# Holding the next block's squares behind ScalarE's evictions in a hybrid GLA/pooling layer pair

## The chip, the core and the metric

The kernel runs on one core of one Trainium2 chip. That core has a matmul engine (PE, with PEld for its weight loads), VectorE (DVE), ScalarE (ACT), GpSimd (POOL) and a queue on SyncE (SP) that issues the DMAs. The engines run side by side, each through its own list of instructions in a fixed order, and wait for each other by semaphores. The metric is the time of one execution in device microseconds (us); lower is better.

## The reference, cut to what matters

Two layers run over 2176 tokens (128 of a prompt, 2048 of a sample) with 1024 channels, in float32. Layer 0 is a gated linear attention (GLA) beside a spatial gating unit, layer 1 a pooling mixer beside a short convolution. Both begin with a norm over the channels of each token, and the change touches only how the first layer's norm is scheduled:

```python
def rmsnorm(x, g):
    xf = x.astype(jnp.float32)
    y = xf * lax.rsqrt(jnp.mean(xf * xf, axis=-1, keepdims=True) + EPS)
    return (y * g.astype(jnp.float32)).astype(x.dtype)
...
        shift, scale, gate = adaln(cond, w_ada[l], b_ada[l])
        h = rmsnorm(x, norm_g[l]) * (1.0 + scale) + shift
...
            out, s_f, s_b = mix_even(h @ w_in_even[j], j, gla_init[j][0], gla_init[j][1])
```

For every token the squares of its 1024 channels have to be summed before the first product with `w_in_even` can begin.

## The kernel before, in words

Tokens lie along the free axis and channels on the 128 partitions, in KT = 8 slabs of 128 channels. Every float32 product is made of three passes (`mm3`): each operand is split into a rounded part (`hi`, `hh`) and a rest (`lo`, `hl`), and hi*hi, hi*lo and lo*hi are summed in PSUM. The split is made by ScalarE (L220, L405) and VectorE or GpSimd (L221, L406).

Layer 0 runs in four blocks of tokens, here called block 0 to 3 (512, 512, 512 and 640 tokens). They begin in the trace at about 27, 217, 398 and 575 us, and layer 0's projections end near 640 us. A block (`block1`) does, in this order: `make_h` for the 8 slabs (L405 on ACT writes `ring_hh`, L406 on DVE writes `ring_hl`); a token-major product of 272 columns (`gemm_tok(0, ...)`) whose tiles of 128 tokens are taken out of PSUM by DVE (L760, L761, the low-rank gate) and ACT (L764, `gl_v`); the q and k products (L777); another token-major product (L792); two products for the gating unit (`gl`: L806 on DVE, L809 on ACT with the sum of squares); then the channel-major products of the gates (L320 to L326, L845, L850). PSUM tiles of these products come from one pool of two buffers (`pg_g`), so the third tile of a product waits until the first has been taken out.

Beside these products run side jobs, advanced by one step at each `tick()`, that is after every second tile or every channel-major product. The GLA of each 128-token tile is one (`gla_tile`, L524 to L682): a chain over ACT (L552), DVE (L557, L568) and POOL (L568) with small matmuls (L580, L586, L605, L613), a large exponential on ACT (L623), DVE products with it (L627 to L634), and at its end a small tile `gl_ub` with one buffer: DVE writes a column of it (L673), ACT the rest (L674), SP stores it (L676), and the next tile's L673 waits for that store. The gating unit's mixer is another side job (L813 to L833), in which POOL scales four tiles (L821).

`prep_x` (L434) is the side job of the change. For the next block it loads the 8 slabs of x (L443, into `ring_xk`, 8 buffers, each free once `make_h` of the present block has read it), has ACT square them (L306 for the first, straight into `tmp_acc`; L309 for the seven others, into `tmp_px`, 4 buffers), adds them up (L310, on POOL for the blocks 1 to 3, on DVE for block 0), takes the reciprocal root (`rstd`, L286) and scales x by it (`make_t`, L390 on DVE).

The written order is not the order on the engines. The framework (`schedule_with_timeline_sim=True`, L1782) plays the program through a model of the engines and lets an instruction take an engine as soon as, in that model, its inputs and buffers are there; what is written earlier goes first among those that are ready. So a square whose slab has come in may be placed on ACT ahead of an eviction that was written before it. Once the lists are made they are fixed, and on the chip an instruction waits for the one ahead of it on its engine.

## Time and profile before

| what | value |
|---|---|
| median of 3 runs | 1852.43 us (1844.92, 1853.93, 1852.43) |
| profiled execution, its own time | 1848.17 us |
| its span | 1846.4 us |
| PE busy | 94% of the span |
| DVE, ACT, POOL busy | 65%, 45%, 40% |

The profiled execution's span is 1.8 us shorter than its time; what lies around the span is not touched here. A row of the timeline gives start, busy time, engine, source line, operation, output and inputs, and in brackets how long the engine had sat idle before it and what ended that. A row of the stretches gives, for a window of time, its length and the busy time of PE, PEld, DVE, ACT and POOL in it, each with its count of instructions, the granted PE clock as a share of 2.4 GHz, the share of the DMA engines and GB/s. Matmuls are pipelined, so a row's duration is longer than the distance between two starts.

### The profile page before, as it was taken

The page shows a single profiled execution, that of the slowest core. Times are in us where ns is not written, and L with a number is a line of the kernel's source. Part 1 is how long each engine was busy: PE and PEld are TensorE (multiplying, and loading weights), DVE is VectorE, ACT ScalarE, POOL GpSimd, SP SyncE. Part 2 cuts the span into 40 slices and gives each one's busy share as a digit, 9 for nine tenths or more (in the row PEclk, how much of TensorE's full clock was granted, in tenths as well). Part 3 has the DMA queues.
Part 4 walks back from the last instruction along what each step waited for, and adds up shares of the span by engine and source line. Part 5 has one row for each costly group of instructions (what it writes and reads, how often), then busy time and mean ns, then how long its engine had stood idle before and what let it go on. Part 6 is the DMA issues. An engine that isn't in the chain of part 4 may idle for free. (4 is left out here: it accounts for less than half of the span.)

```text
span 1846.4 us, 39586 instructions
## 1 busy us (share of the span) xinstructions
PE 1729.9 (94%) x15115; PEld 1585.2 (86%) x15115; DVE 1198.2 (65%) x2288; ACT 837.7 (45%) x1795; POOL 744.6 (40%) x793
## 2 busy tenths in 40 slices
PE   5998999999999999999999798899999999999996
PEld 4876788878888988987799787889998999999996
DVE  5457805860687079567766899996768375937653
ACT  4544524552455156345445454554445354534531
POOL 0432422241323024255555777764346234522322
PEclk9998999999999999999999899999999999999998
DMA  9767756575654535557554576598977697669753
GB/s 332 278 229 274 264 201 242 191 234 208 229 184 152 208 138 178 168 182 237 179 167 135 189 255 218 193 307 274 329 231 231 208 323 241 219 193 328 240 181 126
DMA packets 217629, 410.58 MB, mean 222 GB/s; under 512 B 24544, under 2 KB 70368, under 8 KB 217440
## 3 DMA queue, kind: packets, MB, share of 16 engines
q1 hardware_dynamic: 217440, 408.06, 66.0%
q8 instruction: 119, 1.95, 0.4%
q14 instruction: 70, 0.57, 0.1%
HBM read 312.13 MB, written 95.83 MB: 221 GB/s over the span
## 5 line engine op out<-in xcount | busy, mean ns | idle before, releaser
L251 PE MATMUL pg_g<-t_t,wh_hi 128*128 128x272 f32 (+1 forms) x1920 | 375.9, 293 | 16.5 <-ACT tu_U L1485 6.2
L251 PEld LDWEIGHTS pg_g<-t_t,wh_hi 128*128 128x128 f32 x1920 | 304.9, 191 | 20.1 <-ACT tu_U L1485 6.6
L251 PE MATMUL pg_g<-t_t,wh_lo 128*128 128x280 f32 (+1 forms) x960 | 275.9, 292 | 10.0 <-DVE wh_lo L221 7.9
L251 PE MATMUL pg_g<-ring_hh,wp_hi 128*128 128x512 f32 (+2 forms) x632 | 234.6, 371 | 2.9 <-DVE tmp_ev L845 2.6
L251 PE MATMUL pg_g<-ring_hh,wp_lo 128*128 128x512 f32 (+2 forms) x632 | 229.5, 363 | 0.6 <-DMA wp_lo<-dr_w16l 0.6
L251 PE MATMUL pg_g<-ring_hl,wp_hi 128*128 128x512 f32 (+2 forms) x632 | 229.9, 364 | 0.0
L220 ACT ACTIVATE wh_hi<-wh_raw 128x512 fp32r<-128x512 f32 x202 | 126.5, 628 | 172.9 <-PE pg_g L251 117.0
L251 PEld LDWEIGHTS pg_g<-t_t,wh_lo 128*128 128x128 f32 x960 | 181.5, 191 | 12.3 <-DVE wh_lo L221 9.3
L310 POOL TENSOR_TENSOR tmp_acc<-tmp_acc,tmp_px 128x512 f32<-128x512 f32 (+5 forms) x83 | 113.9, 1372 | 159.5 <-ACT tmp_px L309 136.3
L251 PE MATMUL pg_g<-wp_hi,ring_hh 128*128 128x256 f32 (+1 forms) x528 | 157.4, 298 | 9.8 <-ACT gl_v L764 5.5
L251 PE MATMUL px_x<-t_t,wh_hi 128*128 128x272 f32 (+1 forms) x768 | 155.1, 296 | 5.4 <-DVE tmp_ev L1308 3.7
L221 DVE TENSOR_TENSOR wh_lo<-wh_raw,wh_hi 128x512 fp32r<-128x512 f32 x147 | 128.8, 878 | 44.6 <-ACT wh_hi L220 35.8
L251 PE MATMUL pg_g<-wp_hi,ring_hl 128*128 128x256 f32 (+1 forms) x528 | 153.1, 291 | 2.1 <-DVE ring_hl L406 2.0
L251 PE MATMUL pg_g<-wp_lo,ring_hh 128*128 128x256 f32 (+1 forms) x528 | 152.7, 290 | 0.0
L251 PEld LDWEIGHTS pg_g<-ring_hh,wp_hi 128*128 128x128 f32 x632 | 120.9, 191 | 23.9 <-DVE tmp_ev L845 3.0
L568 POOL TENSOR_TENSOR gl_Z<-gl_Z 128x128 f32<-128x128 f32 x170 | 82.6, 505 | 145.1 <-DVE gl_Z L568 102.1
L251 PEld LDWEIGHTS pg_g<-ring_hh,wp_lo 128*128 128x128 f32 x632 | 120.8, 191 | 17.2 <-issue 0.8
L251 PE MATMUL pg_g<-o_oh,wh_hi 128*128 128x272 f32 (+2 forms) x448 | 130.1, 291 | 5.2 <-ACT o_oh L220 2.0
L251 PEld LDWEIGHTS pg_g<-ring_hl,wp_hi 128*128 128x128 f32 x632 | 120.7, 191 | 14.6 <-issue 0.5
L251 PE MATMUL pg_g<-o_oh,wh_lo 128*128 128x272 f32 (+2 forms) x448 | 130.1, 291 | 2.5 <-DVE wh_lo L221 1.4
L251 PE MATMUL pg_g<-o_ol,wh_hi 128*128 128x272 f32 (+2 forms) x448 | 130.2, 291 | 2.0 <-DVE o_ol L221 2.0
L251 PEld LDWEIGHTS px_x<-t_t,wh_hi 128*128 128x128 f32 x768 | 123.4, 192 | 7.8 <-DVE tmp_ev L1308 3.2
(302 smaller groups left out, 4333.0 us busy)
## 6 DMA issues: line engine op xcount, KB each, us to landing
wh_raw<-in_w_dram SPq DMA_DIRECT2D x132, 256.0 KB, 3.7
wh_hi<-dr_hl SPq DMA_DIRECT2D x108, 256.0 KB, 3.7
wh_lo<-dr_hl SPq DMA_DIRECT2D x108, 256.0 KB, 4.0
wp_raw<-in_w_ada_dram SPq DMA_DIRECT2D x32, 512.0 KB, 5.3
wh_hi<-dr_wo SPq DMA_DIRECT2D x48, 256.0 KB, 4.7
wh_lo<-dr_wo SPq DMA_DIRECT2D x48, 256.0 KB, 5.0
dr_hl<-wh_hi SPq DMA_DIRECT2D x36, 256.0 KB, 3.4
dr_hl<-wh_lo SPq DMA_DIRECT2D x36, 256.0 KB, 2.7
```

What stands on the lines that cost most here:

```text
L220: act(out=hi, in_=src, func=AF.Copy)
L221: (eng or lo_engine()).tensor_tensor(out=lo, in0=src, in1=hi.bitcast(F32), op=ALU.subtract)
L251: mm(out=out, lhsT=a, rhs=b, start=start and i == 0, stop=stop and i == n - 1, skip_group_check=resumed)
L310: eng.tensor_tensor(out=acc, in0=acc, in1=sq, op=ALU.add)
L568: (dve if i >= 2 or s < 4 else gps).tensor_tensor(out=dst, in0=dst, in1=bc(src), op=ALU.add)
```

## The change

`add_square` now returns the ACT instruction of the square. Each eviction by ACT in the first half of `block1` (L764, L777, L792, L809 by the numbers of before) is remembered in `evicted`, and for the blocks 1 to 3 each square is given an order-only dependency (`NoSync`: no semaphore) on the eviction that was written last before it: on ACT it can't be placed ahead of that one. In the text of `prep_x` the square of slab k - 4 is now written behind the load of slab k; for block 0 the code is as before.

```diff
--- before.py
+++ after.py
@@ -209,6 +209,14 @@
     ctile = const(cT, [P, KT, 2], "ct")
     ident = const(ident_d, [P, P], "ident")
 
+    evicted = [None]
+
+    def in_order(i):
+
+        if evicted[0] is not None:
+            tc.add_manual_dep(i.ins, evicted[0].ins.name, mybir.DependencyInfo(
+                mybir.DependencyClass.NoSync, mybir.DependencyReason.DATA), reason="order")
+
 
     lo_ctr = [0]
 
@@ -303,11 +311,12 @@
 
     def add_square(acc, x, n, first, eng, inplace=False):
         if first:
-            act(out=acc, in_=x, func=AF.Square)
+            i = act(out=acc, in_=x, func=AF.Square)
         else:
             sq = x if inplace else px_tile(n)
-            act(out=sq, in_=x, func=AF.Square)
+            i = act(out=sq, in_=x, func=AF.Square)
             eng.tensor_tensor(out=acc, in0=acc, in1=sq, op=ALU.add)
+        return i
 
     def sigmoid_(x, s):
         act(out=s, in_=x, func=AF.Exp, scale=-1.0)
@@ -436,14 +445,26 @@
         n = P * len(TILES[bi])
         acc = tmp.tile([P, 640], F32, tag="acc", bufs=1)[:, 0:n]
         xb[bi] = []
-        for k in range(KT):
+        def x_in(k):
             x = xk_tile(n)
             xb[bi].append(x)
             for c0, t0, w in cols(bi):
                 load(out=x[:, c0:c0 + w], in_=xT[k, :, t0:t0 + w])
-            add_square(acc, x, n, k == 0, gps if bi else dve)
-            if k % 2:
-                yield 1
+
+        if bi:
+            for k in range(KT + 4):
+                if k < KT:
+                    x_in(k)
+                if k >= 4:
+                    in_order(add_square(acc, xb[bi][k - 4], n, k == 4, gps))
+                if k % 2:
+                    yield 1
+        else:
+            for k in range(KT):
+                x_in(k)
+                add_square(acc, xb[bi][k], n, k == 0, dve)
+                if k % 2:
+                    yield 1
         yield 1
         r = tmp.tile([P, 640], F32, tag="r", bufs=1)[:, 0:n]
         yield from rstd(acc, n, r, bi == 0)
@@ -761,7 +782,7 @@
             dve.tensor_tensor(out=l4[:, :, 2, :], in0=lr, in1=hi.bitcast(F32), op=ALU.subtract)
             for j in (0, 3):
                 gps.tensor_copy(out=l4[:, :, j, :], in_=hi.bitcast(F32))
-            act(out=v[i][:, 0:240], in_=o[:, 32:272], func=AF.Copy)
+            evicted[0] = act(out=v[i][:, 0:240], in_=o[:, 32:272], func=AF.Copy)
             lr_t(i - 1)
 
         def lr_t(i):
@@ -774,7 +795,7 @@
 
         def qk0(c, a, b, o):
             for i in range(a // P, b // P):
-                act(out=qk[i][:, c // 2, c % 2, :], in_=o[:, i * P - a:(i + 1) * P - a],
+                evicted[0] = act(out=qk[i][:, c // 2, c % 2, :], in_=o[:, i * P - a:(i + 1) * P - a],
                     func=AF.Copy, scale=0.125 if c < 2 else 1.0)
 
         if bi == 0:
@@ -789,7 +810,7 @@
             if c == c0:
                 lr_t(nt - 1)
         for i, o in gemm_tok(1, 272, h, nt, bi == 0):
-            act(out=v[i][:, 240:512], in_=o, func=AF.Copy)
+            evicted[0] = act(out=v[i][:, 240:512], in_=o, func=AF.Copy)
         for i in range(nt):
             if TILES[bi][i] == 1:
                 Sf[0] = gl.tile([P, 2, P], F32, tag="Sf", bufs=3)
@@ -806,7 +827,7 @@
                 dve.tensor_copy(out=vs[:, i, 2 * u:2 * u + 2, :],
                                 in_=o.rearrange("p (a b) -> p a b", a=2))
                 junk = nw_tile(256)
-                act(out=junk, in_=o, func=AF.Square, accum_out=sq[:, i, u:u + 1])
+                evicted[0] = act(out=junk, in_=o, func=AF.Square, accum_out=sq[:, i, u:u + 1])
 
         def mix():
             v5, a5, r5 = (tmp.tile([P, 5], F32, tag=f"s{i}", bufs=2)[:, 0:nt] for i in range(3))
```

The lists of the engines differ between some 40 us and the end of layer 0's blocks; POOL, SP, DVE and ACT have the same rows as before from there on. The lines of the new file are shifted: L314 and L317 are the squares (L306, L309 before), L318 their sum (L310), L785 the eviction L764, L830 the eviction L809, L781 and L782 the pair L760 and L761, L694 to L697 the handling of `gl_ub` (L673 to L676), L644 is L623, L648 to L655 are L627 to L634, L842 is L821, L589 is L568 and L561 is L540.

ScalarE at the start of block 1, before: `tmp_acc` and `tmp_px` are the squares of block 2's x, `gl_v` the evictions of block 1's first product, `tmp_ev` a gate of block 0, `gl_ub` the GLA tile that is stored.

```order
L306 ACTIVATE tmp_acc_3371<-ring_xk_3372 128x512
L314 ACTIVATE tmp_ev_2619<-tmp_ev_2619 128x512
L674 ACTIVATE gl_ub_2638<-ps_s_2625 128x2x128
L309 ACTIVATE tmp_px_3377<-ring_xk_3375 128x512
L315 ACTIVATE tmp_ev_2619<-tmp_ev_2619 128x512
L309 ACTIVATE tmp_px_3460<-ring_xk_3458 128x512
L309 ACTIVATE tmp_px_3465<-ring_xk_3463 128x512
L764 ACTIVATE gl_v_2752<-pg_g_2784 128x240
L309 ACTIVATE tmp_px_3548<-ring_xk_3546 128x512
L764 ACTIVATE gl_v_2753<-pg_g_2815 128x240
```

The same place after the change:

```order
L322 ACTIVATE tmp_ev_2619<-tmp_ev_2617 128x512
L323 ACTIVATE tmp_ev_2619<-tmp_ev_2619 128x512
L644 ACTIVATE gl_Z_2379<-gl_Z_2379 128x1024
L695 ACTIVATE gl_ub_2638<-ps_s_2625 128x2x128
L324 ACTIVATE tmp_ev_2619<-tmp_ev_2619 128x512
L785 ACTIVATE gl_v_2752<-pg_g_2784 128x240
L785 ACTIVATE gl_v_2753<-pg_g_2815 128x240
L785 ACTIVATE gl_v_2754<-pg_g_2865 128x240
```

All eight squares have left this place (the L306 and three L309 above, four L309 behind), and the exponential of a GLA tile (L644, L623 before) has come in, which before stood ahead of `make_h`.

VectorE at the start of block 2, before: `gl_M` and `gl_D` belong to a GLA tile, `tmp_lrh` and `gl_lr` are VectorE's part of taking out the first product's tiles, `gl_ub` is the column that waits for a store.

```order
L589 TENSOR_TENSOR gl_M_4886<-pm_m_4821,gl_mask_525 128x640
L593 TENSOR_REDUCE gl_D_4589<-gl_M_4886 128x64 x2
L760 CAST tmp_lrh_4976<-pg_g_4951 128x32
L761 TENSOR_TENSOR gl_lr_0_4_547<-pg_g_4951,tmp_lrh_4976 128x2x16
L673 COPY gl_ub_5250<-gl_dec_5147 128x2
L760 CAST tmp_lrh_5007<-pg_g_4982 128x32
L761 TENSOR_TENSOR gl_lr_1_5_548<-pg_g_4982,tmp_lrh_5007 128x2x16
```

The same place after the change:

```order
L655 TENSOR_TENSOR gl_Z_4576<-gl_qk_2759,gl_Z_4576 128x512
L415 SCALAR_TENSOR_TENSOR ring_hl_4928<-ring_xk_3703,cst_ada_104,ring_hh_4927 128x512
L610 TENSOR_TENSOR gl_M_4886<-pm_m_4821,gl_mask_525 128x640
L614 TENSOR_REDUCE gl_D_4585<-gl_M_4886 128x64 x2
L694 COPY gl_ub_5250<-gl_dec_5147 128x2
L781 CAST tmp_lrh_4976<-pg_g_4951 128x32
L782 TENSOR_TENSOR gl_lr_0_4_547<-pg_g_4951,tmp_lrh_4976 128x2x16
L781 CAST tmp_lrh_5007<-pg_g_4982 128x32
L782 TENSOR_TENSOR gl_lr_1_5_548<-pg_g_4982,tmp_lrh_5007 128x2x16
```

The column of `gl_ub` has moved from behind the first tile's pair to ahead of it; behind block 1's last `ring_hl` the four instructions L648 to L655 stand in the same way ahead of the first pair.

GpSimd in block 1, where it scales the mixer's four tiles (`sg_vs`), before: `gl_Z` is the GLA chain.

```order
L540 MEMSET gl_Z_3694 128x512
L821 TENSOR_SCALAR sg_vs_3278<-sg_vs_3278,tmp_s_95_3795 128x512 x4
L568 TENSOR_TENSOR gl_Z_3694<-gl_Z_3694 128x32x4 x2
L568 TENSOR_TENSOR gl_Z_3694<-gl_Z_3694 128x16x8 x2
L568 TENSOR_TENSOR gl_Z_3694<-gl_Z_3694 128x8x16 x2
L568 TENSOR_TENSOR gl_Z_3694<-gl_Z_3694 128x4x32 x2
```

The same place after the change:

```order
L318 TENSOR_TENSOR tmp_acc_3371<-tmp_acc_3371,tmp_px_3541 128x512
L318 TENSOR_TENSOR tmp_acc_3371<-tmp_acc_3371,tmp_px_3700 128x512
L318 TENSOR_TENSOR tmp_acc_3371<-tmp_acc_3371,tmp_px_3705 128x512
L318 TENSOR_TENSOR tmp_acc_3371<-tmp_acc_3371,tmp_px_3781 128x512
L561 MEMSET gl_Z_3682 128x512
L318 TENSOR_TENSOR tmp_acc_3371<-tmp_acc_3371,tmp_px_3784 128x512
L842 TENSOR_SCALAR sg_vs_3278<-sg_vs_3278,tmp_s_93_3789 128x512 x4
L318 TENSOR_TENSOR tmp_acc_3371<-tmp_acc_3371,tmp_px_3913 128x512
L589 TENSOR_TENSOR gl_Z_3682<-gl_Z_3682 128x32x4 x2
L318 TENSOR_TENSOR tmp_acc_3371<-tmp_acc_3371,tmp_px_3916 128x512
L589 TENSOR_TENSOR gl_Z_3682<-gl_Z_3682 128x16x8 x2
```

The seven sums (`tmp_acc`) now stand here, five of them ahead of the scaling; before they stood at the start of the block. In SP's list the loads of x stand where they stood, within two places.

## Rows read from the trace of the kernel before

**Rows 1.** This is the page's line of busy times: us, share of the span and instructions of each engine.

```profile
PE 1729.9 (94%) x15115; PEld 1585.2 (86%) x15115; DVE 1198.2 (65%) x2288; ACT 837.7 (45%) x1795; POOL 744.6 (40%) x793
```

**Rows 2.** This is the view by stretches; the columns are explained above the change.

```profile
0.00:640.00 640.00, 600.03 (x6170) 502.26 (x6171) 355.52 (x813) 277.98 (x616) 178.68 (x241) 0.98 0.67 232
...
140.00:180.00 40.00, 34.09 (x346) 24.99 (x339) 30.25 (x64) 18.68 (x33) 8.46 (x8) 0.88 0.79 271
...
229.00:240.00 11.00, 8.77 (x82) 8.34 (x80) 1.72 (x10) 5.63 (x12) 10.30 (x14) 0.84 0.77 287
...
300.00:340.00 40.00, 39.64 (x500) 32.05 (x500) 25.46 (x61) 18.37 (x44) 11.90 (x15) 1.00 0.70 236
...
380.00:420.00 40.00, 36.18 (x486) 31.11 (x485) 24.60 (x56) 21.59 (x41) 21.56 (x30) 1.00 0.70 233
```

**Rows 3.** This is the view of waits, PE's from 0 to 640 us: who waited for whom, us in total, times, the longest.

```profile
PE pg_g L251 <- DVE ring_hl L406: 2.0, 5, 0.6
...
PE pg_g L251 <- ACT ring_hh L405: 1.7, 1, 1.7
...
PE pg_g L251 <- ACT gl_v L764: 5.5, 2, 3.3
```

**Rows 4.** This is the timeline of PE: the starts of block 0, block 1 and block 2, and two later matmuls of block 1 and one of block 2.

```profile
44.26 0.49 PE L251 MATMUL pg_g<-wp_hi,ring_hh 128*128 128x272 f32 x1 [1.72 <-ACT ring_hh L405]
...
231.86 0.39 PE L251 MATMUL pg_g<-wp_hi,ring_hh 128*128 128x272 f32 x1 [2.23 <-ACT gl_v L764]
...
232.25 0.43 PE L251 MATMUL pg_g<-wp_hi,ring_hl 128*128 128x272 f32 x1
...
235.61 0.29 PE L251 MATMUL pg_g<-wp_hi,ring_hl 128*128 128x272 f32 x1
...
411.38 0.39 PE L251 MATMUL pg_g<-wp_hi,ring_hh 128*128 128x272 f32 x1 [3.31 <-ACT gl_v L764]
...
411.61 0.29 PE L251 MATMUL pg_g<-wp_lo,ring_hh 128*128 128x272 f32 x1
```

**Rows 5.** This is the timeline of ACT, at the starts of block 0 and block 1.

```profile
42.99 0.61 ACT L306 ACTIVATE tmp_acc<-ring_xk 128x512 f32<-128x512 f32 x1
...
227.60 0.63 ACT L306 ACTIVATE tmp_acc<-ring_xk 128x512 f32<-128x512 f32 x1 [2.72 <-DMA ring_xk<-in_xT_dram]
...
228.66 0.37 ACT L674 ACTIVATE gl_ub<-ps_s 128x256 f32<-128x256 f32 x1
...
230.91 0.63 ACT L309 ACTIVATE tmp_px<-ring_xk 128x512 f32<-128x512 f32 x1 [0.34 <-POOL tmp_acc L310]
...
231.45 0.35 ACT L764 ACTIVATE gl_v<-pg_g 128x240 f32<-128x240 f32 x1
```

**Rows 6.** This is the timeline of ACT, at the start of block 2.

```profile
404.27 0.74 ACT L309 ACTIVATE tmp_px<-ring_xk 128x640 f32<-128x640 f32 x1 [1.73 <-DMA ring_xk<-in_xT_dram]
...
406.10 0.37 ACT L674 ACTIVATE gl_ub<-ps_s 128x256 f32<-128x256 f32 x1
...
409.13 0.74 ACT L309 ACTIVATE tmp_px<-ring_xk 128x640 f32<-128x640 f32 x1 [2.15 <-DMA ring_xk<-in_xT_dram]
...
410.98 0.35 ACT L764 ACTIVATE gl_v<-pg_g 128x240 f32<-128x240 f32 x1
```

**Rows 7.** This is the timeline of DVE, at the starts of block 1 and block 2.

```profile
218.06 0.17 DVE L627 COPY gl_dec<-gl_Z 128x2 f32<-128x2 f32 x1 [1.19 <-ACT gl_Z L623]
...
219.41 3.40 DVE L406 SCALAR_TENSOR_TENSOR ring_hl<-ring_xk,cst_ada,ring_hh 128x512 fp32r<-128x512 f32 x5
...
229.13 0.20 DVE L760 CAST tmp_lrh<-pg_g 128x32 fp32r<-128x32 f32 x1
...
406.52 0.18 DVE L760 CAST tmp_lrh<-pg_g 128x32 fp32r<-128x32 f32 x1
...
411.69 0.17 DVE L673 COPY gl_ub<-gl_dec 128x2 f32<-128x2 f32 x1 [4.76 <-DMA dr_ub<-gl_ub]
...
411.77 0.18 DVE L760 CAST tmp_lrh<-pg_g 128x32 fp32r<-128x32 f32 x1
```

**Rows 8.** This is the timeline of SP, the store of `gl_ub` at the start of block 2.

```profile
408.28 0.33 SPq L676 DMA_DIRECT2D dr_ub<-gl_ub  x1
```

**Rows 9.** This is the timeline of DVE and ACT at the start of block 3, behind which no block follows and so no squares stand.

```profile
586.59 0.16 DVE L673 COPY gl_ub<-gl_dec 128x2 f32<-128x2 f32 x1
...
587.93 0.19 DVE L760 CAST tmp_lrh<-pg_g 128x32 fp32r<-128x32 f32 x1
...
588.44 0.69 ACT L764 ACTIVATE gl_v<-pg_g 128x240 f32<-128x240 f32 x2 [3.29 <-DVE tmp_lrh L760]
```

**Rows 10.** This is the timeline of POOL and DVE in block 0: sums on POOL, and two slabs of `make_h` on DVE, one beside them and one behind.

```profile
46.65 4.35 POOL L310 TENSOR_TENSOR tmp_acc<-tmp_acc,tmp_px 128x512 f32<-128x512 f32 x3 [2.29 <-ACT tmp_px L309]
...
48.00 1.85 DVE L406 SCALAR_TENSOR_TENSOR ring_hl<-ring_xk,cst_ada,ring_hh 128x512 fp32r<-128x512 f32 x1
...
51.20 0.74 DVE L406 SCALAR_TENSOR_TENSOR ring_hl<-ring_xk,cst_ada,ring_hh 128x512 fp32r<-128x512 f32 x1
```

**Rows 11.** This is POOL's view of the tile `tmp_acc` from 0 to 640 us (duration in ns: least, median, most), and POOL's timeline in block 1.

```profile
L310 POOL TENSOR_TENSOR tmp_acc<-tmp_acc,tmp_px x21: 1264/1292/1623, 46.6 to 418.9; 128x512 f32<-128x512 f32 x14, 128x640 f32<-128x640 f32 x7
...
313.40 6.68 POOL L821 TENSOR_SCALAR sg_vs<-sg_vs,tmp_s 128x512 f32<-128x512 f32 x4
...
320.06 1.12 POOL L568 TENSOR_TENSOR gl_Z<-gl_Z 128x128 f32<-128x128 f32 x2
```

## The prediction

> **What bounds the kernel now.** I read the page's busy times first: PE is busy for 94% of the span [rows 1], so time is won only where PE stands idle or runs at its lower clock. Then the stretches: in the first 640 us, to which the change is confined, PE is busy for 600.0 us, so 40 us are idle, some of them before the first product [rows 2]. Then PE's waits there. Those with which the moved squares can have to do are three groups: 5.5 us in two waits for `gl_v` (L764), 1.7 us in one wait for `ring_hh`, 2.0 us in five waits for `ring_hl` [rows 3]. The timeline of PE gives them their places: 1.72 us at the start of block 0, 2.23 us at the start of block 1, 3.31 us at the start of block 2 [rows 4].
>
> The timeline of ACT shows why the two long ones last. At the start of block 1 the first square sits 2.72 us on a load of x, with the store tile `gl_ub` behind it, and the eviction L764 begins only when three more squares are done, one of them held by GpSimd's sum; it begins at 231.45 and PE goes on at 231.86 [rows 4, 5]. At the start of block 2 two squares sit 1.73 and 2.15 us on loads, and L764 begins at 410.98, PE at 411.38 [rows 4, 6]. So ACT's fixed order, and not a lack of ACT time, is the cause. Block 3 has no squares behind it: there L764 begins 0.5 us after DVE's L760, so it waits for nothing but its own tile [rows 9].
>
> An idle PE costs more than its gap where the granted clock falls behind it. After the 2.23 us of block 1 a matmul row of 272 columns lasts 0.43 us, from 235.61 on 0.29 us [rows 4], and the granted clock of 229 to 240 us averages 0.84 [rows 2], that is 1.2 GHz for about 3.5 us (11 x 0.16 x 2), a loss of some 1.8 us. After the longer gap of block 2 it doesn't fall: 1.00 over 380 to 420 us [rows 2], and the next row lasts 0.29 us [rows 4]. So I count a fall as likely but not sure.
>
> **The change part by part.** The sum is made against the profiled execution, 1848.2 us.
>
> Block 0: the first square stands ahead of the second half of `make_h` on ACT, from 42.99 for 0.61 us [rows 5], and PE waits 1.72 us for that half [rows 4]. With the square gone it is 0.5 us (the rows overlap a little). Bounds: 0, if the products wait for `ring_hl` instead; 2.3, if the clock that falls here too (its rows last 0.4 us and more) stays up. I take 0.5. Beside it the sums leave GpSimd here, which matters for DVE (below).
>
> Block 1: all squares leave the place between `make_h` and L764 (the first two fences of the change). The eviction is then bound by DVE's L760 and L761, which ACT follows as in block 3. DVE's L760 came at 229.13 [rows 7]. In its way come L627 to L634, four instructions that take 1.35 us (218.06 to 219.41) and stood ahead of the first `ring_hl` [rows 7]; they now stand behind the last. But for the same reason `ring_hl` can begin that much earlier, and it no longer waits 1.19 us for the exponential [rows 7]. I count this as even: L760 at 229.1, L764 0.5 us later and 0.4 us for it and its signal, as now, PE at 230.0 in place of 231.9: 1.9 us gained and 0.3 us of wait left, so the clock should stay up, which is 1.8 us more. Together 3.7. Bounds: 0.5, if the 1.35 us come on top and the clock falls all the same; 4.0, the whole wait and the fall.
>
> Block 2: here something else is late next. On DVE the column of `gl_ub` (L673) now stands ahead of the first L760 (the second pair of fences). Before, it waited 4.76 us for the store of the GLA tile ahead of it and then ran at 411.69, but the first tile's pair had gone at 406.52, so only the second tile was held, until 411.77 [rows 7]. Now both are held, with everything behind them on DVE, and PE's third tile waits for them. The store is issued at 408.28 [rows 8], after ACT has written the tile at 406.10 [rows 6], and lands 3.4 us later (408.28 to 411.69). ACT gets to the tile sooner: it waited 1.73 us for x and squared for 0.74 [rows 6], 2.5 us together. The exponential L623 now stands in between, so I count 2.3 of it. With a store that much earlier L673 runs at 409.4, L760 at 409.5, L764 0.5 later, and PE goes on at 410.4 in place of 411.4: 1.0 us of the 3.3. Bounds: -1.2, if the store isn't earlier at all (411.8 for L760, 412.6 for PE); 3.3. In block 3, with no loads in the queue, L673 waits for nothing [rows 9], which shows that it need not be late.
>
> What takes on the squares: eight in each of three blocks move to the last evictions L809 of the gating unit. ACT is busy for 18.4 of the 40 us there (300 to 340) [rows 2], and the loads came in long before, so ACT has room. GpSimd is the tighter one. It took the seven sums while DVE was all but idle (1.72 of 11 us) [rows 2]; now five of them stand ahead of the scaling L821, and two among the first steps of the GLA chain (the third pair of fences). At 1.29 us each [rows 11] four of these come after the last L809 and push L821, which began at 313.40, back by up to 5.2 us, less what ACT's own order gave it in wait; I estimate 2 to 3. The first step of the chain behind it, at 320.06 [rows 11], moves by that and one sum more, up to 4 us. PE is idle there for only 0.4 of 40 us [rows 2], and the fixed order moves the GLA's small matmuls back as well, so most of it is hidden by the products in between; if that cover is gone it is 4 us in each of three blocks, 12 in all.
>
> The sums also slow DVE. `ring_hl` lasts 1.85 us beside a sum and 0.74 us without [rows 10]. The Trainium skill has a rule for this (SBUF — State Buffer, section "Who interferes with whom"): a VectorE instruction with two inputs in SBUF and a GpSimd instruction that reads SBUF hold a common port in turn, each for its whole length. The trace agrees, 1.85 against 0.74 us; by the rule as it stands each of the seven sums could hold DVE for its 1.29 us, 9 us in a block, and the sum below would end as in the second rival. By the rows, each collision costs DVE 1.1 us. In block 0 that is won back by `make_h` (one or two collisions, 1 to 2 us of DVE, on which PE waits little). In the new place DVE is busy for 25.5 of 40 us [rows 2], so perhaps four of seven sums collide, 4 us of DVE out of 14.5 idle. For crowding on GpSimd and DVE together I charge 1.5 us; bounds 0 and 16 (12 for the late chain, 4 for DVE).
>
> Between 140 and 180 us PE stands idle for 5.9 us, and the granted clock of 0.88 costs another 4.8 (40 x 0.12) [rows 2]. These are waits of the GLA and of the conditioning weights in the fixed order, which the change shuffles here more than anywhere. It can remove or add; I take 0, bounds -8 (won) and +6 (lost).
>
> The loads: in SP's list they stand where they stood. That half of the change I cost at nothing.
>
> Sum: 0.5 + 3.7 + 1.0 - 1.5 = 3.7 us won of 1848.2, or 0.2%. The profiled execution is one of four that are known: with the three runs shown (1844.9, 1852.4, 1853.9) their mean is 1849.9, and the median of the runs is 4.3 above the profiled one. I set the base at 1849.9 and predict 1846.
>
> **The rivals.**
>
> First, the waits change owner: DVE's pairs, held by L627 to L634 in block 1 and by the store in block 2, come as late as the evictions did. For it speaks that L673 has waited 4.76 us here already; against it that ACT's first wait for x, which made the store late, is gone. Then 0.5 + 0.5 + 0 - 1.5 is no gain: 1850.
>
> Second, slower: the late GLA chain. Five sums ahead of L821 and the collisions with DVE delay the chain by 4 us or more, and PE, whose order is fixed, stands at the first small matmul of the chain in each block. The point from which it decides is the cover: the wait shows only when the chain is later than the model that made the order takes it to be. Against it, the model knows the sums, and PE waited 0.4 us in this stretch before. Price: up to 12 to 16 us, less the 5.2 won at the block starts, and in the middle some 8 lost: 1858.
>
> Third, more is won than the starts: with fewer sums in the way of `make_h` and another order, the 10.7 us (5.9 + 4.8) lost from 140 to 180 us go largely. For it speaks that waits of this kind are missing in the same stretch of blocks 1 and 2 (1.00 from 300 to 340 us [rows 2]); against it, the change doesn't touch their cause. Then 3.7 + 8: 1838.
>
> That the order does not do what it says is ruled out for the squares by the lists, and holds for the loads.
>
> **How the numbers follow.** The forecast of 1846 has 0.5, the first rival 0.2, the second and the third 0.15 each. The likeliest's own range is 1841 to 1850. The range that should hold 8 in 10 reaches to the third rival with its own spread below and to the middle of the second above, and takes in that runs of one kernel lie 9 us apart: 1834 to 1858. About 0.5%, 9.3 us, is what a measurement of this kernel can tell from no change. Below 1843 on a base of 1852.4 lie most of the third rival and a fifth of the forecast: faster 0.25. Above 1861.7 lies the upper part of the second: slower 0.12. The rest, 0.63, is within.
>
> **What would show it.** Right: PE's wait for `gl_v` at the start of block 1 under 0.6 us and no fall of the clock behind it; at block 2 a wait of 2 to 2.6 us whose releaser is no longer a late ACT but DVE's L760 behind `gl_ub`; L405 at block 0 half a microsecond earlier; PE's idle time from 300 to 340 us under 1.5 us. Wrong: a wait of 2 us or more at block 1 with DVE as the releaser (first rival), PE idle at L586, L605 or L641 for over 2 us in the stretches after the moved sums (second), or the stretch from 140 to 180 us with a clock of 1.00 (third). A difference behind 640 us, where nothing is moved, would show that I have taken the change's reach too small.

## The result and the profile after

The changed kernel takes 1862.9 us, the median of 6 runs (1859.52 to 1868.42); the kernel before took 1849.66 beside it. The ratio over all runs (not exactly that of the two medians) is 1.0077, with a 95% interval of 1.0059 to 1.0094: slower by 14 us (11 to 17). The forecast was 1846, the range 1834 to 1858: the sign was wrong and the time lies outside. The profiled execution took 1859.52 us.

First the page's busy times, which answer to [rows 1], then the stretches of [rows 2], with two more; of these the one from 180 to 229 us is shown for the kernel before too.

```profile
PE 1733.8 (93%) x15115; PEld 1587.7 (85%) x15115; DVE 1216.6 (65%) x2288; ACT 835.9 (45%) x1795; POOL 751.6 (40%) x793
```

```profile
0.00:640.00 640.00, 592.34 (x6058) 493.85 (x6059) 369.83 (x813) 274.23 (x608) 186.85 (x241) 0.97 0.65 227
140.00:180.00 40.00, 38.09 (x405) 28.43 (x405) 32.91 (x70) 20.97 (x40) 16.80 (x19) 0.96 0.74 254
180.00:229.00 49.00, 44.59 (x483) 36.34 (x482) 42.86 (x73) 28.14 (x49) 21.06 (x20) 0.93 0.86 301
229.00:240.00 11.00, 8.72 (x123) 8.05 (x122) 5.84 (x17) 0.63 (x2) 2.84 (x7) 0.84 0.65 213
300.00:340.00 40.00, 37.79 (x513) 30.73 (x513) 26.11 (x58) 22.41 (x52) 21.73 (x22) 1.00 0.67 230
380.00:420.00 40.00, 36.56 (x424) 31.06 (x423) 31.64 (x70) 20.58 (x41) 16.00 (x21) 0.96 0.68 228
580.00:600.00 20.00, 16.38 (x293) 13.52 (x295) 18.82 (x37) 12.97 (x28) 8.38 (x10) 1.00 0.40 145
```

```profile
180.00:229.00 49.00, 47.74 (x477) 39.01 (x476) 43.20 (x78) 28.08 (x52) 21.35 (x25) 0.99 0.75 258
```

PE is idle for 7.7 us more of the first 640 us than before (640 - 592.34 against 640 - 600.03). Over the whole execution PE has the same 15115 matmuls; the span is 11.3 us longer (1857.7 against 1846.4), and PE's busy time 3.9 us (1733.8 against 1729.9). So most of the loss is waiting, and the rest is the same work taking longer, beside a granted clock of 0.97 in place of 0.98 in these 640 us. PE's waits from 0 to 640 us show for what:

```profile
PE pg_g L259 <- DVE ring_hl L415: 6.6, 11, 1.8
...
PE ps_s L792 <- POOL gl_lr L784: 3.7, 2, 2.2
PE ps_s L662 <- DVE sg_vs L851: 3.5, 1, 3.5
...
PE ps_s L792 <- DVE gl_ub L694: 2.3, 1, 2.3
PE ps_s L682 <- ACT gl_o L674: 2.2, 1, 2.2
PE ps_s L671 <- ACT gl_kT L665: 2.2, 1, 2.2
PE pg_g L259 <- ACT ring_hh L414: 2.1, 1, 2.1
PE ps_s L848 <- ACT gl_kT L665: 2.1, 1, 2.1
```

The wait for `gl_v`, 5.5 us in [rows 3], is gone, as the change meant. In its place stand waits of 2 to 3.5 us each, for the transposed `lr` at the block starts (L792), for the mixer's rows (`sg_vs`), for the GLA chain (`gl_o`, `gl_kT`), and for `ring_hl`, 6.6 us against 2.0.

To see where the time goes I measure from block to block, between the last evictions of q and k (L777 before, L798 after), on ACT's timeline: before, then after.

```profile
74.29 0.76 ACT L777 ACTIVATE gl_qk<-pg_g 128x128 f32<-128x128 f32 x4
...
266.16 0.78 ACT L777 ACTIVATE gl_qk<-pg_g 128x128 f32<-128x128 f32 x4 [4.66 <-PE pg_g L251]
...
445.38 0.79 ACT L777 ACTIVATE gl_qk<-pg_g 128x128 f32<-128x128 f32 x4 [5.46 <-PE pg_g L251]
...
634.10 0.45 ACT L777 ACTIVATE gl_qk<-pg_g 128x128 f32<-128x128 f32 x2 [2.25 <-PE pg_g L251]
```

```profile
73.30 0.76 ACT L798 ACTIVATE gl_qk<-pg_g 128x128 f32<-128x128 f32 x4
...
268.11 0.79 ACT L798 ACTIVATE gl_qk<-pg_g 128x128 f32<-128x128 f32 x4 [4.66 <-PE pg_g L259]
...
450.01 0.79 ACT L798 ACTIVATE gl_qk<-pg_g 128x128 f32<-128x128 f32 x4 [5.45 <-PE pg_g L259]
...
648.69 0.45 ACT L798 ACTIVATE gl_qk<-pg_g 128x128 f32<-128x128 f32 x2 [2.25 <-PE pg_g L259]
```

End to end, block 0 to 1 takes 191.9 us before and 194.8 after, 1 to 2 takes 179.2 and 181.9, 2 to 3 takes 188.4 and 198.3. All three are longer, the last by ten. Behind block 3 nothing is lost: from its last q and k eviction to the end of the span it is 1211.9 us before and 1208.6 after. PE's timeline at the start of block 3 after, where [rows 9] showed nothing late:

```profile
592.32 0.39 PE L259 MATMUL pg_g<-wp_hi,ring_hl 128*128 128x272 f32 x1 [0.87 <-DVE ring_hl L415]
...
598.70 0.52 PE L259 MATMUL pg_g<-wp_hi,ring_hl 128*128 128x272 f32 x2 [1.83 <-DVE ring_hl L415]
...
601.77 0.48 PE L792 MATMUL ps_s<-cst_ident,gl_lr 128*128 128x128 f32 x1 [1.51 <-POOL gl_lr L784]
```

VectorE is late there. It is busy for 18.82 of the 20 us from 580 to 600; the first `ring_hh` comes at 585.46, and the first L781 at 601.12, 15.7 us behind it (before 12.1, from 575.83 to the 587.93 of [rows 9]); whether the loss lies in that, the experiments show. A level of the GLA chain of block 2's last tile (L578, L589) stands among its `ring_hl`:

```profile
586.21 1.02 DVE L415 SCALAR_TENSOR_TENSOR ring_hl<-ring_xk,cst_ada,ring_hh 128x512 fp32r<-128x512 f32 x2 [0.70 <-ACT ring_hh L414]
587.14 0.69 DVE L578 TENSOR_TENSOR gl_L<-gl_qk,gl_L 128x512 f32<-128x512 f32 x1
587.75 0.49 DVE L589 TENSOR_TENSOR gl_Z<-gl_Z 128x128 f32<-128x128 f32 x2
...
601.12 0.28 DVE L781 CAST tmp_lrh<-pg_g 128x32 fp32r<-128x32 f32 x2
```

What has moved ahead of that shows best on PE's timeline of block 0: the row sums of the next x (L283 and L284 before, L291 and L292 after) among the mixer's tiles (L827, L848). Before, then after:

```profile
128.12 1.16 PE L827 MATMUL ps_s<-sg_wst,sg_vs 128*128 128x128 f32 x8
147.28 0.40 PE L283 MATMUL ps_s<-tmp_nw,cst_ones_r 128*128 128x512 f32 x1
...
151.37 1.05 PE L827 MATMUL ps_s<-sg_wst,sg_vs 128*128 128x128 f32 x8
...
172.23 1.16 PE L827 MATMUL ps_s<-sg_wst,sg_vs 128*128 128x128 f32 x8
```

```profile
167.34 1.05 PE L848 MATMUL ps_s<-sg_wst,sg_vs 128*128 128x128 f32 x8
...
170.79 0.50 PE L291 MATMUL ps_s<-tmp_nw,cst_ones_r 128*128 128x512 f32 x1
```

Before, the row sum is behind the mixer's first tile; after, behind its last, 97 us behind the last q and k eviction of the block in place of 72 (170.79 - 74.1, 147.28 - 75.1). With it goes the scaling of x on VectorE (L390, L399); in block 2 it begins 101 us behind that eviction in place of 79:

```profile
525.06 7.49 DVE L390 SCALAR_TENSOR_TENSOR ring_xk<-ring_xk,cst_gs,tmp_r 128x512 f32<-128x512 f32 x16
```

```profile
551.98 0.74 DVE L399 SCALAR_TENSOR_TENSOR ring_xk<-ring_xk,cst_gs,tmp_r 128x512 f32<-128x512 f32 x1
...
553.07 5.13 DVE L399 SCALAR_TENSOR_TENSOR ring_xk<-ring_xk,cst_gs,tmp_r 128x128 f32<-128x128 f32 x11
```

The reason is in the diff, and the prediction passed over it. The loop over the loads runs KT + 4 times in place of KT and yields at every second, so the preparation has two steps more ahead of its row sums. That this alone moves them, the first experiment shows.

### The profile page after: what moved, and what is told of

Its sections match the earlier page's. It is cut to its first block, busy times and chain, and to the rows that moved or that the text cites. A ratio compares the mean times of both kernels' runs of the same rounds, so it can differ in the third digit from the quotient of the medians.

```text
span 1857.7 us, 39591 instructions
## 1 busy us (share of the span) xinstructions
PE 1733.8 (93%) x15115; PEld 1587.7 (85%) x15115; DVE 1216.6 (65%) x2288; ACT 835.9 (45%) x1795; POOL 751.6 (40%) x793
## 5 line engine op out<-in xcount | busy, mean ns | idle before, releaser
L259 PE MATMUL pg_g<-ring_hl,wp_hi 128*128 128x512 f32 (+2 forms) x632 | 229.1, 362 | 0.0
L318 POOL TENSOR_TENSOR tmp_acc<-tmp_acc,tmp_px 128x512 f32<-128x512 f32 (+5 forms) x83 | 113.5, 1367 | 164.3 <-ACT tmp_px L317 157.3
L589 POOL TENSOR_TENSOR gl_Z<-gl_Z 128x128 f32<-128x128 f32 x170 | 85.1, 519 | 143.7 <-DVE gl_Z L589 105.3
```

Of the source, the lines that this page charges most:

```text
L259: mm(out=out, lhsT=a, rhs=b, start=start and i == 0, stop=stop and i == n - 1, skip_group_check=resumed)
L318: eng.tensor_tensor(out=acc, in0=acc, in1=sq, op=ALU.add)
L589: (dve if i >= 2 or s < 4 else gps).tensor_tensor(out=dst, in0=dst, in1=bc(src), op=ALU.add)
```

## The experiments

Two theories. A: the two added steps cost, by the late row sums and what hangs on them. B: the held squares and their sums cost, where they now stand among the mixer and the GLA chain. The lists settle a third, that the distance between load and square costs: squares written four loads late, with no hold and no added step, leave every engine's list as it was, row for row but for the numbers of buffers. So the distance does nothing by itself; with the hold it does something else, as the second group of runs shows. The differences below are worked out from each run's ratio to the kernel before, times 1849 us, with the 95% interval.

**The two halves apart.** The first kernel is the one before with two steps more, the second the changed one without them.

```diff
 two_steps_only (against the kernel before)
-        yield 1
+        for _ in range(3 if bi else 1):
+            yield 1
         r = tmp.tile([P, 640], F32, tag="r", bufs=1)[:, 0:n]
 hold_without_steps (against the changed kernel)
-                if k % 2:
+                if k % 2 and k < KT:
                     yield 1
```

> The kernel before, with nothing of the change but its length: the preparation of the next x yields two times more ahead of its reciprocal root, as it does in the changed kernel. No square is held, no load is issued earlier. Theory A (the two more steps are the loss: they push everything behind them, the row scale, the modulation of x and by them the GLA chains of the last tiles, into the starts of the next blocks): PE waits for ring_hl and for the transposed lr at the start of block 3 (2 to 3 us each, as in the changed kernel), the gl_v waits of blocks 1 and 2 stay, and the time is 8 to 16 us above the kernel before. Theory B (the loss comes from the squares and sums that now run among the mixer and the GLA chain): the time is within 3 us of the kernel before.

> The changed kernel, without the two more yields: the squares are still written four loads late and held behind ScalarE's evictions, but the preparation is as long as in the kernel before. Theory A: the gl_v waits are gone, PE does not wait at the start of block 3, and the time is 1 to 6 us below the kernel before (the 5.5 us of gl_v waits and their clock, less crowding). Theory B: the PE waits of the changed kernel in block 0 (3.5 us at L662 for sg_vs, 2.2 us at L682) and at 519 us stay, and the time is 6 to 13 us above the kernel before.

Measured: 1855.7, ratio 1.0050 (1.0033 to 1.0068), +9.2 us, as theory A said; and 1854.6, ratio 1.0034 (1.0020 to 1.0049), +6.3 us, as theory B said. In two_steps_only the row sum of block 0 stands behind the mixer's last tile, as in the changed kernel (at 172.63 us). Both theories hold, each for its part, and the parts add up to 15.5 against the 14.2 of the whole change. In two_steps_only the start of block 3 is that of the changed kernel, wait by wait, though no square has moved:

```profile
591.54 0.40 PE L251 MATMUL pg_g<-wp_hi,ring_hl 128*128 128x272 f32 x1 [0.88 <-DVE ring_hl L406]
...
597.91 0.52 PE L251 MATMUL pg_g<-wp_hi,ring_hl 128*128 128x272 f32 x2 [1.85 <-DVE ring_hl L406]
...
600.99 0.46 PE L772 MATMUL ps_s<-cst_ident,gl_lr 128*128 128x128 f32 x1 [1.51 <-POOL gl_lr L764]
```

In hold_without_steps the row sums are back in their place but their input is late: GpSimd's timeline in block 2, and PE's wait.

```profile
500.63 6.30 POOL L842 TENSOR_SCALAR sg_vs<-sg_vs,tmp_s 128x512 f32<-128x512 f32 x4
...
507.67 1.62 POOL L318 TENSOR_TENSOR tmp_acc<-tmp_acc,tmp_px 128x640 f32<-128x640 f32 x1
...
514.94 1.59 POOL L318 TENSOR_TENSOR tmp_acc<-tmp_acc,tmp_px 128x640 f32<-128x640 f32 x1
```

```profile
518.60 0.44 PE L291 MATMUL ps_s<-tmp_nw,cst_ones_r 128*128 128x384 f32 x1 [2.91 <-ACT tmp_nw L228]
```

Three of the sums stand behind the scaling of the mixer's rows (L842). The last ends at 516.5, and only then can ACT and GpSimd split the result for PE, which stands idle for 2.91 us. GpSimd's split begins at 518.62, 69 us behind the block's last q and k eviction; in the kernel before it began 44 us behind it (490.45 - 446.2).

**Where the squares stand.** hold_at_each_load writes each square behind its load again; hold_first_products takes, beyond that, the hold from the later evictions.

```diff
 hold_at_each_load (against the changed kernel)
-            for k in range(KT + 4):
-                if k < KT:
-                    x_in(k)
-                if k >= 4:
-                    in_order(add_square(acc, xb[bi][k - 4], n, k == 4, gps))
+            for k in range(KT):
+                x_in(k)
+                in_order(add_square(acc, xb[bi][k], n, k == 0, gps))
 hold_first_products (against hold_at_each_load)
-            evicted[0] = act(out=v[i][:, 240:512], in_=o, func=AF.Copy)
+            act(out=v[i][:, 240:512], in_=o, func=AF.Copy)
-                evicted[0] = act(out=junk, in_=o, func=AF.Square, accum_out=sq[:, i, u:u + 1])
+                act(out=junk, in_=o, func=AF.Square, accum_out=sq[:, i, u:u + 1])
```

> The order alone: each square is written right behind its load as in the kernel before, and held behind the last eviction written. Four squares come to stand between the sets of the mixer's rows instead of eight behind them. Theory A: as the kernel without the two steps, 1 to 6 us below the kernel before. Theory B: nearly the same crowding, 5 to 12 us above it. A third theory (the loads of x, or their distance from the squares, matter): PE waits for a DMA in front of a square's reader somewhere in blocks 1 to 3, over 1 us each.

> Each square is written behind its load, and held only behind the evictions of the first product and of the q and k products, so that the squares fall into the stretch from 240 to 300 us (and 420 to 470 us), where VectorE, ScalarE and GpSimd are under a third busy, and are over when the GLA chains begin. Both theories: the gl_v waits are gone and no crowding comes in their place, 3 to 7 us below the kernel before. If it is no faster than the kernel without the two steps, the squares' place matters little, which speaks for A; if it is faster by 5 us or more, B holds for a part.

Measured: -1.8 us (-4.1 to +0.4), which lies where theory A had it and not 5 to 12 us above, where B had it; and +3.9 us (+1.3 to +6.7), a miss for both theories, which had it 3 to 7 us below. So the hold alone costs nothing that can be told, and no wait of PE for the loads of x, the third theory of that expectation, is in its trace. Two steps earlier, the same held squares cost 8 us less than in hold_without_steps: a square is held behind the eviction written last before it, so writing it four loads late ties it to a later eviction. On GpSimd all seven sums of block 2 now stand ahead of the scaling of the mixer's rows (L840 here), and the split begins 56 us behind the last q and k eviction (495.80 - 439.4) in place of 69:

```profile
484.46 3.39 POOL L318 TENSOR_TENSOR tmp_acc<-tmp_acc,tmp_px 128x640 f32<-128x640 f32 x2 [3.59 <-ACT tmp_px L317]
...
488.80 7.03 POOL L840 TENSOR_SCALAR sg_vs<-sg_vs,tmp_s 128x512 f32<-128x512 f32 x4
...
495.80 1.00 POOL L229 TENSOR_TENSOR tmp_nw<-tmp_acc,tmp_nw 128x384 fp32r<-128x384 f32 x1
```

By blocks, from one profile of each:

| us between the last q and k evictions | 0 to 1 | 1 to 2 | 2 to 3 |
|---|---|---|---|
| before | 191.9 | 179.2 | 188.4 |
| changed | 194.8 | 181.9 | 198.3 |
| two_steps_only | 194.8 | 181.5 | 193.2 |
| hold_without_steps | 191.1 | 180.2 | 195.5 |
| hold_at_each_load | 188.7 | 176.5 | 194.2 |
| hold_first_products | 196.8 | 177.8 | 188.4 |
| hold_mixed (below) | 189.6 | 176.4 | 188.4 |
| mixed_with_steps (below) | 191.2 | 178.7 | 194.0 |

hold_at_each_load wins 3 us twice, and loses 5.8 from block 2 to 3, where block 3's wider squares (640 columns) are made; there hold_first_products is even. So each block was given the better of the two: the second entry of `evicted`, which block 3's squares follow, is set by the first product and by q and k alone.

```diff
 hold_mixed (against hold_at_each_load)
+        e = evicted[bi == NB - 1]
 ...
+            evicted[0] = evicted[1] = act(out=v[i][:, 0:240], in_=o[:, 32:272], func=AF.Copy)
 ...
+                evicted[0] = evicted[1] = act(out=qk[i][:, c // 2, c % 2, :], ...
 mixed_with_steps (against hold_mixed)
-        yield 1
+        for _ in range(3 if bi else 1):
+            yield 1
```

> The row sums stand where they stood before (no step added). The squares of blocks 1 and 2 are held as in hold_at_each_load, those of block 3 as in hold_first_products. By the evictions of q and k, hold_at_each_load was 3.1 us shorter than the kernel before from block 0 to 1 and 2.8 us from block 1 to 2, and 5.8 us longer from block 2 to 3; hold_first_products was even from block 2 to 3. If these stretches add, as both theories have it once the place of the squares is chosen block by block, the time is 4 to 7 us below the kernel before and the stretch from block 2 to 3 is 188 to 190 us. If the 5.8 us do not hang on where block 3's squares stand, it is 0 to 2 us below as hold_at_each_load was.

> hold_mixed with the two more yields ahead of the row sums, and nothing else. If the two steps cost what they cost by themselves whatever the squares do (two_steps_only lay 9.2 us above the kernel before by its ratio of 1.005), this is 7 to 11 us above hold_mixed: 1847 to 1852 us, about the kernel before. If the held squares hide them or are needed for them, it is within 3 us of hold_mixed. By stretches of the q and k evictions: the two steps are to add 2 to 3 us from block 0 to 1 and 4 to 5 from block 2 to 3.

Measured: hold_mixed 1840.6, ratio 0.9957 (0.9941 to 0.9973), 8.0 us below the kernel before and the fastest here that computes everything (4 to 7 were expected; the interval is 5.0 to 10.9); its three stretches are those of the two kernels that it is put together from, within 1 us. mixed_with_steps 1849.2, +0.9 us (-2.4 to +4.3): the two steps cost 8.9 us here too, 5.6 of it from block 2 to 3 by the profiles. Its start of block 3 has the three waits again (0.88, 1.82, 1.42 us). The steps' price does not hang on the squares.

**What of the two steps costs.** Both kernels leave out the scaling of x by its row scale for blocks 1 to 3, one with the two steps and one without.

```diff
 steps_no_scale (against two_steps_only), before_no_scale (against the kernel before)
         for k in range(KT):
-            make_t(xb[bi][k], k, 0, r, conds0(bi))
+            if not bi:
+                make_t(xb[bi][k], k, 0, r, conds0(bi))
```

> two_steps_only with the multiplication of x by its row scale left out for blocks 1 to 3 (8 to 16 VectorE instructions of 0.35 to 0.74 us in each block, 5 to 8 us of VectorE). If the two steps cost because they put these instructions, 26 us later, among the GLA chains of a block's last tiles, the time falls by 6 to 10 us against two_steps_only, and the stretch between the q and k evictions of blocks 2 and 3 falls from 193 to 187 to 189 us. If they cost by the row sum's place in TensorE's order and in the two buffers it shares with the GLA tiles, it falls by under 4 us.

> The kernel before with the same multiplication left out for blocks 1 to 3: the control of steps_no_scale. Both theories: within 4 us of the kernel before, since these instructions stand in stretches where VectorE has room. If steps_no_scale is within 2 us of this one, the multiplication's place is the two steps' cost; if it stays 6 us or more above, the row sum's place is. The list of ScalarE's instructions shows here, too, GLA instructions between the ring_hh of the starts of blocks 2 and 3; if these alone cost time, this kernel is 5 us or more above the kernel before.

Measured: +1.1 us (-1.3 to +3.5), and -5.2 us (-7.4 to -2.8). Without the scaling the steps still cost 6.3 us, with it 9.2; the intervals are too wide to tell these apart. By the expectation on record, 6 us or more would put the cost on the row sum's place and not on the scaling's. The profiles say more of one part: from block 2 to 3 the two take 189.0 and 189.1 us, where two_steps_only took 193.2, so most of that stretch's loss goes with the scaling, which the steps put among the last tiles' GLA instructions. The rest falls from block 0 to 1 (192.7 and 187.3). One profile of each can't settle that: behind block 3, where the edit changes nothing, the same two differ by 2.8 us (1214.1 and 1211.3). What the rest hangs on, the row sum's place or another thing, stays open. Nor is the late VectorE at the start of block 3 the loss by itself: from the first `ring_hh` to the first `tmp_lrh` it is 15.7 us in both of these kernels too, also in the one without the steps, and both stretches take 189 us.

**What of the late squares costs.** Two kernels leave out GpSimd's sums of squares (a row sum is then that of the first square). The edit reaches further than its expectations say: 83 instructions are gone from GpSimd, the 21 of blocks 1 to 3 and 62 behind layer 0. Two other kernels have the 21 on VectorE, and leave the 62 alone.

```diff
 hold_no_sums (against hold_without_steps), before_no_sums (against the kernel before)
-            eng.tensor_tensor(out=acc, in0=acc, in1=sq, op=ALU.add)
+            if eng is not gps or inplace:
+                eng.tensor_tensor(out=acc, in0=acc, in1=sq, op=ALU.add)
 hold_sums_dve (against hold_without_steps)
-                    in_order(add_square(acc, xb[bi][k - 4], n, k == 4, gps))
+                    in_order(add_square(acc, xb[bi][k - 4], n, k == 4, dve))
 mixed_sums_dve (against hold_mixed)
-                in_order(add_square(acc, xb[bi][k], n, k == 0, gps), bi)
+                in_order(add_square(acc, xb[bi][k], n, k == 0, dve), bi)
```

> hold_without_steps with GpSimd's seven sums of squares of each block 1 to 3 left out (the row sum is then that of the first square alone; every square is still computed and held; everything behind is as before). If the sums on GpSimd are what the late squares cost (they end at 131 us in block 0 and 516 us in block 2, and the row sum's split waits for them), the loss of 7 us goes: within 2 us of the kernel before or below it, with no PE wait for the split at 518 us. If ScalarE's squares among the evictions and the GLA chain cost it, the loss stays: 4 to 8 us above the kernel before.

> The kernel before with GpSimd's seven sums of squares of blocks 1 to 3 left out, the row sum being that of the first square alone: the control of hold_no_sums (which fell by some 20 us against hold_without_steps, to 13 us below the kernel before). If the sums cost because of where the held squares put them, this one gains little, 0 to 5 us against the kernel before (the squares wait less for their two buffers, so the gl_v waits of blocks 1 and 2 shrink). If sums on GpSimd cost some 13 us or more wherever they stand, it is 10 to 14 us below the kernel before, and hold_no_sums shows only that.

> hold_without_steps with the seven sums of each of blocks 1 to 3 on VectorE in place of GpSimd. If it is GpSimd's queue that makes the late squares dear (its sums at 1.3 to 1.6 us each among the scaling of the mixer's rows and the split of the row sum), the row sums' split is ready earlier and the time falls to within 2 us of the kernel before. If any engine's time among the mixer and the GLA chain is as dear, it stays 4 to 10 us above.

> hold_mixed with the sums of blocks 1 to 3 on VectorE. Of the squares held behind the first products and the mixer's evictions the sums stand in stretches where VectorE is a third busy or less, so under the theory of GpSimd's queue it is 0 to 4 us below hold_mixed (1836 to 1841 us); under the other it is 2 to 6 us above, as VectorE feeds the GLA chain from the end of those stretches on.

Measured: hold_no_sums -13.3 us (-16.3 to -10.4), 19.6 below hold_without_steps; its control -3.9 (-7.2 to -0.6). Part of both is won behind layer 0: from block 3's last q and k eviction to the end of the span it is 1203.3 us in place of 1209.4, and 1203.7 in place of 1211.9. As both lack the same 62, this part drops out of the difference between them, 15.7 us, give or take 5 by the three intervals. That much of the sums is their place, or the other order that the lists take without them, and not the sums. hold_sums_dve -1.5 us (-4.6 to +1.7), 7.8 below the same kernel with GpSimd. GpSimd's timeline of block 2 there:

```profile
493.07 7.04 POOL L842 TENSOR_SCALAR sg_vs<-sg_vs,tmp_s 128x512 f32<-128x512 f32 x4
...
500.47 1.02 POOL L229 TENSOR_TENSOR tmp_nw<-tmp_acc,tmp_nw 128x384 fp32r<-128x384 f32 x1
```

The block runs 7.7 us earlier as a whole (its last q and k eviction ends at 441.8 in place of 449.5), so only distances from there count: the scaling begins 51 us behind in both, but the split 59 in place of 69. What the late squares cost is thus, for a good part (7.8 us), row sums that wait for sums queued behind the mixer's scaling on GpSimd. mixed_sums_dve is a miss for both accounts, of which the worse had it 6 us above hold_mixed: +5.2 us (+1.5 to +8.9), 13 above hold_mixed, with PE waiting 3.9 us in block 0 for VectorE's `gl_L`. So VectorE is no better place in itself; it helped where GpSimd's queue was in the way, and did harm where it was not. Why so much, one profile, of an execution 4.6 us below the median, doesn't settle.

## Why the prediction was wrong

- **The loads** ("That half of the change I cost at nothing"): this is the step that failed. The loads do stand where they stood in SP's list, and their distance by itself does nothing. But the half of the change that issues them ahead also lengthens the preparation by two yields, measured at 9.2 us, and 8.9 on another base; and under the hold it ties each square to a later eviction, measured at 8 us (hold_without_steps against hold_at_each_load). The hold without that half stands at -1.8 us, with 3.7 won inside its interval; so this half, costed at 0, is worth some 16 us, all of the loss. I costed the text's purpose in place of what its loop does.
- **Crowding** (1.5 us charged, bounds 0 to 16): right in kind, mis-sized. It was read from the changed kernel's own lists, so the late squares were in it: without the two steps the sum still said 3.7 us won, and hold_without_steps lost 6.3, 10 us more. That kernel has the `gl_v` waits removed as hold_mixed has, and lies 14 us above it (6.3 above and 8.0 below the kernel before), so that much lies between these two places of the squares. The upper bound for the late chain (12, and 4 for DVE's collisions) held it; the reason for not taking it, that the order moves the GLA's matmuls back too and the products hide the delay, did not hold. Each part of the chain came late once: L662 by 3.5 us, L682, L671 and L848 by 2.1 to 2.2.
- **Block 1** (3.7 us won): the wait for `gl_v` is gone as said, but PE waits 2.28 us at 234.25 for the transposed `lr`, released by DVE's `gl_ub` column, and the granted clock from 229 to 240 us is 0.84 as before. The prediction counted the moved L648 to L655 as even and L781 at 229.1; it came at 233.60, behind the last of them (L655, at 233.00). This is the first rival's change of owner. With hold_mixed's order 1.5 us of wait is left, and the stretch wins 2.2: the term was of the right kind, for another order.
- **Block 2** (1.0 us won): PE waits 2.23 us at 414.74 in place of 3.31, 1.1 us less where 1.0 was forecast. The releaser is GpSimd's copy of `lr`, one step behind DVE's L781, and `gl_ub` waited 1.34 us for its store in place of 4.76, so this mechanism was right. But the start came 3.4 us late as a whole (414.74 against 411.38), and here the clock does fall (below), which the forecast did not count.
- **Block 0** (0.5 us won): can't be told. PE waits 2.11 us for `ring_hh` at its start, against 1.72, with no square ahead of it; in hold_mixed and hold_at_each_load, where none stands there either, 1.15 and 2.10, so this wait differs by a microsecond from profile to profile.
- **From 140 to 180 us** (0, bounds -8 and +6): PE idles 1.9 us in place of 5.9 and the clock rises from 0.88 to 0.96, some 7 us won. But from 180 to 229 us it idles 4.4 against 1.3 and the clock falls from 0.99 to 0.93, 6 us lost. A stretch read alone would have borne out the third rival.
- **The second rival** (the late GLA chain, 1858, given 0.15) was nearest. Its place was right for the part of the late squares, and PE is idle for 2.21 us from 300 to 340 us in place of 0.36; it lacked the row sums and the two steps.
- **What would show it**: the list named the test that decided (PE idle for over 2 us at L641, which is L662 now and waits 3.5 us), but for the step that failed it looked at SP's list only, and no sign was named for row sums or scaling.

## What to carry to other kernels

A generator that yields to a scheduler has a length as well as a content: count its steps before and after the change, and find on TensorE's list what stands behind the last one, here the row sums, before any part is called free. Moving a chain's first instructions behind other work moves its end, so place them where every engine that the chain needs still has a gap, block by block (hold_mixed), rather than by one rule. And where an order is fixed, don't count on the products in between to hide a delay: here late links of the chain were waited for where they were planned, 2 to 3.5 us each.

## What the runs showed of the hardware

Two slabs of `ring_hl` on VectorE that took 1.00 us together at 591.53 took 3.02 at 596.89, beside two GpSimd instructions with two inputs (596.12 to 599.77, the changed kernel's timelines of DVE and POOL):

```profile
591.53 1.00 DVE L415 SCALAR_TENSOR_TENSOR ring_hl<-ring_xk,cst_ada,ring_hh 128x512 fp32r<-128x512 f32 x2
...
596.89 3.02 DVE L415 SCALAR_TENSOR_TENSOR ring_hl<-ring_xk,cst_ada,ring_hh 128x512 fp32r<-128x512 f32 x2
```

```profile
596.12 1.98 POOL L335 TENSOR_TENSOR tmp_ev<-tmp_ev,tmp_ev 128x512 f32<-128x512 f32 x1 [9.71 <-DVE gl_M L610]
598.17 1.60 POOL L871 TENSOR_TENSOR tmp_ev<-tmp_ev,tmp_ev 128x512 f32<-128x512 f32 x1
```

That is 1.0 us more for each slab (1.1 in [rows 10]), and it agrees with the rule of the Trainium skill (SBUF — State Buffer, section "Who interferes with whom") that the two engines hold a common port in turn. It was not counted at a block start, where PE waited 1.83 us for these very slabs.

The clock did not follow the length of the gap in these two cases. At the start of block 2, after an idle time of 2.23 us in the changed kernel, rows of 272 columns lasted 0.29 us and then 0.43 us, and the granted clock from 417 to 420 us is 0.52, about the lower level of 1.2 GHz; after 3.31 us in the kernel before there was no such fall [rows 4], and the clock stayed at 1.00 from 380 to 420 us [rows 2].

```profile
414.74 0.33 PE L792 MATMUL ps_s<-cst_ident,gl_lr 128*128 128x128 f32 x1 [2.23 <-POOL gl_lr L784]
...
416.25 0.29 PE L259 MATMUL pg_g<-wp_hi,ring_hh 128*128 128x272 f32 x1
...
416.52 0.43 PE L259 MATMUL pg_g<-wp_hi,ring_hl 128*128 128x272 f32 x1
```
